# Reversed columns in 512-column matmuls and interleaved halves of the pair products' weights

## The chip, the core and the metric

The kernel runs on one core of one Trainium2 chip. The metric is the device time of one execution in microseconds (us); lower is better. Five engines of the core work side by side, each with its own stream of instructions: TensorE (PE, with its weight loads as PEld) multiplies, VectorE (DVE) and ScalarE (ACT) do elementwise work, GpSimd (POOL) does small things, SyncE (SP) issues most transfers (DMA). SBUF is the on-chip working memory, PSUM the memory into which TensorE writes its sums; both have 128 partitions. PSUM is used here as eight banks of 512 fp32 columns per partition.

A matmul here is two instructions: LDWEIGHTS loads a 128 x 128 block (the weights) into the array, MATMUL streams the other operand (the moving one) through it, column by column, and adds the results to columns of PSUM. In Python it is one call, `nc.tensor.matmul(out, weights, moving, ...)`.

## The reference

Two requests of 512 tokens with 1024 features each go through the same trunk of two layers and a final RMSNorm:

```python
for i in range(DEPTH):                        # DEPTH = 2
    h = rms_norm(x, norm_g[i], NORM_EPS)
    if i % N_MIXERS == 0:
        x = x + diff_attention(h, da_w_in[j], ..., da_w_out[j], lambda_init)
    else:
        x = x + bidir_retention(h, ret_w_in[j], ..., ret_w_out[j])
return rms_norm(x, final_norm_g, NORM_EPS)
```

Layer 1 is differential attention: `proj = h @ w_in` (1024 x 8192) gives queries and keys of 16 half heads, values and a gate; the queries and keys are rotated; each of the 8 heads takes the difference of two softmaxes times the values, a norm, the gate, and `@ w_out` (2048 x 1024). Layer 2 is retention in both directions with decays: a projection of 1024 x 6144, rotation, a masked product by chunks, norm, gate and an output projection of 2048 x 1024. All in fp32.

## The kernel before, in words

**Numbers.** A value is split into a rounded part (hi, in the type fp32r, which TensorE multiplies in one pass) and the rest (lo). `hi_of` (L399) makes the first on ScalarE with a copy that casts (L400), `lo_of` (L402) the second on VectorE with a subtraction (L403). A product then takes three matmuls, hi with hi, hi with lo and lo with hi: `PASSES` (L32).

**Projections into the heads.** They are computed with Strassen and Winograd's scheme of seven products of half matrices instead of eight. The transposed and normed activations of both requests are the B operands (`make_b`, L448): tiles `[128, 2, 512]`, hi and lo, which stay in SBUF, some in a large tile `arena` and some in tiles `b`. The projection's weights are the A operands. A `Unit` (L518) is 256 columns of them. `prep` (L551) loads them from HBM into `raw` tiles, combines them as the product asks (L558, into `st`), and splits the result into hi and lo in a `ws` tile; there are seven places for `ws` tiles. `product` (L586) issues the matmuls, `evac` (L627) copies, adds and stores the results.

There are two kinds of units. In a *wide* unit (the values) the activations are the loaded 128 x 128 blocks and the weights are the moving operand, in 256 columns (L609). In a *pair* unit (queries, keys, gates) it is the other way round: the block loaded into the array is 128 columns of the projection's weights, and the activations are the moving operand, all 512 tokens of a request, into a whole bank (`pair`, L596 to L601). One pair product is four k blocks times three passes, 12 matmuls. Its `ws` tile is `[P, 2, 4, n]` (L578): all of hi, then all of lo, each as four blocks of 128 columns. For the queries and keys the weights of a unit are picked by `half_view` (L944) in layer 1 and by `parity_view` (L947, every second column) in layer 2.

**Attention, retention, output.** `scores` (L1107) multiplies queries by keys, 512 key columns in three matmuls per half head (L1116). `av` (L1170) and its like in layer 2 (L1359, L1367, L1315, L1339) have 256 columns. `out_step` (L871) is the output projection: the weighted values are the loaded blocks, 512 columns of the output weights the moving operand, six matmuls to a bank (L891); VectorE adds the bank to the residual (L896). The very last step is done in two halves of 256 columns. Transposes (L606, L716, L815, L1028, L1161) are matmuls by the identity.

**Order.** All of it is recorded first, with a cost for each operation, and `Plan.arrange` (L138) then simulates the engines with these costs, picks for each engine what it issues next, and fixes the order; `Plan.issue` (L232) issues it. The planner knows costs by engine and size, not the direction or step of an access. Places in SBUF are given out by `slot` (L303), which shifts some tiles by 16 or 32 elements.

Of the kernel before, what the change touches and what calls it, by code (L numbers as in the profile page):

```python
# [15 lines left out]
P = 128  # L16
# [237 lines left out]
def trunk_kernel(  # L254
# [7 lines left out]
    nc = tc.nc  # L262
# [34 lines left out]
    def work(tag, shape, bufs, dt=F32, name=None):  # L297
        size = SIZE.get(tag, shape[1])
        return Buf(plan, tag, bufs, lambda i: view(wk, tag, i, size, shape, dt))
# [27 lines left out]
    def ws_t(shape):  # L327
        return work("ws", shape, WS_BUFS, F32R)
# [4 lines left out]
    def st_t(shape, name="st"):  # L333
        return work("st", shape, 3, name=name)
# [18 lines left out]
    def bank(tag, name=None):  # L353
        return Buf(plan, tag, BUFS[tag], lambda i: view(pj if tag == "pj" else sc, tag, i, S, [P, S]))
# [16 lines left out]
    def dve(n, fn, r, w, wait=0.0):  # L371
        plan.op("DVE", 0.07 + 0.00104 * n, fn, r, w, wait=wait)

    def axpy(n, fn, r, w):

        plan.op("DVE", 0.13 + 0.00104 * n, fn, r, w)
# [13 lines left out]
    def pe(cost, fn, r, w, wait=0.0):  # L390
        plan.op("PE", cost, fn, r, w, wait=wait)
# [7 lines left out]
    def hi_of(n, dst, src, r, w):  # L399
        act(n, lambda: nc.scalar.copy(dst(), src()), r, w)  # L400

    def lo_of(n, dst, src, hi, r, w):  # L402
        dve(n, lambda: nc.vector.tensor_tensor(dst(), src(), hi().bitcast(F32), op=ALU.subtract), r, w)  # L403
# [114 lines left out]
    class Unit:  # L518
# [32 lines left out]
        def prep(self, op):  # L551
            x = self.take
            n = 256 if self.wide else P

            def combine(a, b, fn):
                t = st_t([P, 4, n])
                out = ((lambda: self.like(t.t)), t)
                dve(4 * n, lambda: nc.vector.tensor_tensor(out[0](), a[0](), b[0](), op=fn), [a[1], b[1]], [t])  # L558
                return out
            if op == "P1":  # L560
                src = x(0, 0)
            elif op == "P2":
                src = x(0, 1)
            elif op == "P4":
                src = x(1, 1)
            elif op == "P5":
                src = self.s[1] = combine(x(1, 0), x(1, 1), ALU.add)
            elif op == "P6":
                src = self.s[2] = combine(self.s[1], x(0, 0), ALU.subtract)
            elif op == "P3":  # L570
                src = combine(x(0, 1), self.s[2], ALU.subtract)
            else:
                src = combine(x(0, 0), x(1, 0), ALU.subtract)
            if self.wide:
                a, b = ws_t([P, 4, n]), ws_t([P, 4, n])
                hi, lo = ((lambda: a.t), a), ((lambda: b.t), b)
            else:
                s = ws_t([P, 2, 4, n])  # L578
                hi, lo = ((lambda: s[:, 0]), (s, 0)), ((lambda: s[:, 1]), (s, 1))
            hi_of(4 * n, lambda: self.like(hi[0]()), src[0], [src[1]], [hi[1]])  # L580
            lo_of(4 * n, lambda: self.like(lo[0]()), src[0], lambda: self.like(hi[0]()), [src[1], hi[1]], [lo[1]])
            self.ops[op] = (hi, lo)
            if op == "P2" and self.early is not None:
                self.early, self.x = None, {}

        def product(self, op):  # L586
            which = BANK_OF[op]
            n_banks = 2 if self.wide else 1
            opens = op in OPENS
            if opens:  # L590
                self.banks[which] = [bank(self.tags[which], which) for _ in range(n_banks)]
            a, b = self.ops.pop(op), B_OF[op]
            bt = [Bop[b, k] for k in range(4)]
            reads = [q[1] for q in a] + bt

            def pair(ps, ks=range(4)):  # L596
                for k in ks:
                    for i, (u, v) in enumerate(PASSES):
                        nc.tensor.matmul(  # L599
                            ps.t, a[u][0]()[:, k, :], bt[k][:, v, :], start=(opens and k == 0 and i == 0),  # L600
                            stop=(k == 3 and i == 2), skip_group_check=True)  # L601

            def wide(ps, t):
                if self.led and op == "P1" and t == 0:
                    for j in range(NT):
                        nc.tensor.transpose(ps[:, j * P:(j + 1) * P], ident.t, ident.t)  # L606
                for k in range(4):
                    for i, (u, v) in enumerate(PASSES):
                        nc.tensor.matmul(  # L609
                            ps[:, (t % 2) * 256:(t % 2) * 256 + 256], bt[k][:, v, t * P:(t + 1) * P],  # L610
                            a[u][0]()[:, k, :], start=(opens and t % 2 == 0 and k == 0 and i == 0),
                            stop=(k == 3 and i == 2), skip_group_check=True)

            if not self.wide:
                ps = self.banks[which][0]
                if op == "P1" and self in first_units[:2]:
                    for k in range(4):
                        pe(0.7, lambda k=k: pair(ps, (k,)), reads[:2] + [bt[k]], [(ps, k)])
                else:
                    pe(2.79, lambda: pair(ps), reads, [ps])  # L620
                return
            for t in range(NT):
                ps = self.banks[which][t // 2]
                led = self.led and op == "P1" and t == 0
                pe(1.87 if led else 1.43, lambda ps=ps, t=t: wide(ps, t), reads + [ident] * led, [ps])
# [236 lines left out]
    def out_weights(w, h, i):  # L862
        r = raw_t([P, 2, S])
        src = w[h * 256:(h + 1) * 256, i * S:(i + 1) * S].rearrange("(e p) c -> p e c", p=P)
        dma(lambda: r.t, lambda: src, [], [r], 512)
        hi, lo = ws_t([P, 2, S]), ws_t([P, 2, S])
        hi_of(1024, lambda: hi.t, lambda: r.t, [r], [hi])
        lo_of(1024, lambda: lo.t, lambda: r.t, lambda: hi.t, [r, hi], [lo])
        wsn[h, i] = (hi, lo)

    def out_step(w, h, g, t, i, o, rr, last, parts=1):  # L871


        owed[h, g] -= 1
        if (h, i) not in wsn:
            out_weights(w, h, i)
        banks = [bank("pj") for _ in range(parts)]
        u = wsn[h, i]
        x = xN[g, t]
        n = S // parts  # L880
        for p in range(parts):
            here = slice(p * n, (p + 1) * n)
            part = (x, i) if parts == 1 else (x, (i, p))

            ps = banks[p]

            def fn(here=here, ps=ps):
                m = 0
                for e in range(2):
                    for a, b in PASSES:  # L890
                        nc.tensor.matmul(ps[:, here], o[a][:, e, t * P:(t + 1) * P], u[b][:, e, here],  # L891
                                         start=(m == 0), stop=(m == 5))
                        m += 1
            pe(1.39 / parts, fn, [(o[0], t // 2), (o[1], t // 2), *u], [ps])
            half = x[:, i * S + p * n:i * S + (p + 1) * n]
            axpy(n, lambda half=half, here=here, ps=ps: nc.vector.scalar_tensor_tensor(  # L896
                half, ps[:, here], rr[:, t % 2:t % 2 + 1], half, op0=ALU.mult, op1=ALU.add),
                [ps, part, rr], [part])
            if h == NH - 1:
                last(g, t, i, half, n, part, i == 1 and p == parts - 1)  # L900
# [206 lines left out]
    def scores(i):  # L1107
        h, g, t = tiles[i]
        st[i]['s'] = []
        for j in range(2):  # L1110
            s = bank("sc")
            q, k = qk[h, g, j, 0], qk[h, g, j, 1]

            def fn(s=s, q=q, k=k):
                for n, (a, b) in enumerate(PASSES):
                    nc.tensor.matmul(s.t, q[:, a, t * P:(t + 1) * P], k[:, b, :], start=(n == 0), stop=(n == 2))  # L1116
            pe(0.7, fn, [q, k], [s])
            st[i]['s'].append(s)

# [333 lines left out]
    for i in range(N2 + 1):  # L1453
        if i < N2:
            b, c = chunks[i]
# [78 lines left out]
```

## Time and profile before

| what | value |
|---|---|
| median of 3 runs | 1808.89 us (1808.3 to 1814.46) |
| span of the profiled execution, first to last instruction | 1807.0 us |
| the profiled execution's own time | not listed apart; the median is 1.9 us over its span |
| instructions | 27780 |
| granted TensorE clock, mean | 0.999 |
| moved by DMA | 328.81 MB, mean 182 GB/s |

The page lists busy time by engine, the span in 40 slices with a digit for the busy tenths of each, then shares of the chain of work that ended last, and the costliest groups of instructions. In a group, "128*128 128x512" is a 128 x 128 loaded block and 512 moving columns, xN is how many instructions, then come the busy time in us and the mean duration of one in ns, and after the second bar how long its engine sat idle before them. Matmuls overlap: one starts while the one before it drains. The timeline gives start, length and count of runs of equal instructions in us; the chain in order of time gives start and length of each piece. SBUF places do not show in a profile.

### The profile page before, as it was taken

To read this page: it belongs to the slowest core of one execution; us is meant where nothing else is said; L and a number is where in the kernel's file an instruction comes from. 1 tells how busy PE (TensorE), PEld (TensorE's weight loads), DVE (VectorE), ACT (ScalarE), POOL (GpSimd) and SP (SyncE) were. 2 spreads that over 40 slices of the span, in tenths; PEclk is the share of its full clock that TensorE was granted. 3 is DMA by queue.
4 is the path that set the end of the run, shared out by engine and by line. 5 is a ranking of instruction groups with operands and counts; after the bars stand their busy time and mean duration, and the time that the engine had idled before them with its cause. 6 is when DMAs were issued, how large, how long until landed. Compare 5 with 4: busy or idle time off the path is not lost.

```text
span 1807.0 us, 27780 instructions
## 1 busy us (share of the span) xinstructions
PE 1794.9 (99%) x10299; PEld 1558.1 (86%) x10299; DVE 1477.1 (82%) x2319; ACT 895.1 (50%) x1856; POOL 169.5 (9%) x323
## 2 busy tenths in 40 slices
PE   9999999999999999999999999999999999999998
PEld 6789889898988888888888888898989898888887
DVE  7958787778699888888888897787887967888887
ACT  7753444433434565554555866444434355444346
POOL 1000000000000022222322300000000000111113
PEclk9999999999999999999999999999999999999999
DMA  6444455555545685444554524464657559765662
GB/s 217 134 126 137 161 140 178 184 168 155 174 126 175 201 334 198 178 156 159 190 204 140 190 73 146 140 210 146 205 156 228 151 170 396 272 238 182 225 218 94
DMA packets 162767, 328.81 MB, mean 182 GB/s; under 512 B 12724, under 2 KB 76872, under 8 KB 162632
## 3 DMA queue, kind: packets, MB, share of 16 engines
q1 hardware_dynamic: 162304, 326.71, 54.1%
q8 instruction: 81, 1.33, 0.3%
q14 instruction: 54, 0.44, 0.1%
q10 hardware_dynamic: 328, 0.34, 0.1%
HBM read 209.55 MB, written 117.44 MB: 181 GB/s over the span
## 4 chain that ended last, share of the span: by engine, by line
PE 93%; DVE 2%; DMA 2%; ACT 2%; issue 1%; POOL 0%; SPq 0%; POOLq 0%; DVEq 0%; ACTq 0%
PE pj L599 20%; PE pj L891 19%; PE sc L599 10%; PE pj L609 10%; PE o L599 8%; PE o L1181 5%; PE sc L1116 5%; PE sc L609 5%; PE o L609 2%; PE o L1359 2%; PE tp L1161 2%; PE sc L1315 1%; PE o L1367 1%; PE tp L1339 1%; DMA raw<-in_ret_w_out_dram 1%
## 5 line engine op out<-in xcount | busy, mean ns | idle before, releaser
L891 PE MATMUL pj<-ws,arena 128*128 128x512 f32 x1542 | 391.2, 397 | 0.0
L891 PEld LDWEIGHTS pj<-ws,arena 128*128 128x128 f32 x1542 | 277.7, 188 | 52.7
L599 PE MATMUL pj<-b,ws 128*128 128x512 f32 x1080 | 265.0, 392 | 0.0
L599 PEld LDWEIGHTS pj<-b,ws 128*128 128x128 f32 x1080 | 201.4, 188 | 43.0
L403 DVE TENSOR_TENSOR ws<-st,ws 128x512 fp32r<-128x512 f32 (+1 forms) x192 | 147.9, 774 | 74.8 <-ACT ws L400 56.7
L896 DVE SCALAR_TENSOR_TENSOR b<-pj,crr,b 128x512 f32<-128x512 f32 (+1 forms) x257 | 189.9, 744 | 21.4 <-PE pj L891 21.0
L403 DVE TENSOR_TENSOR ws<-raw,ws 128x512 fp32r<-128x512 f32 (+1 forms) x164 | 141.5, 868 | 71.3 <-ACT ws L400 61.0
L400 ACT CAST ws<-st 128x512 fp32r<-128x512 f32 (+1 forms) x192 | 132.4, 693 | 121.4 <-PE pj L599 36.4
L599 PE MATMUL sc<-arena,ws 128*128 128x512 f32 x768 | 186.8, 392 | 0.0
L599 PE MATMUL o<-arena,ws 128*128 128x512 f32 x744 | 180.0, 393 | 1.1 <-ACT m L385 0.6
L599 PEld LDWEIGHTS sc<-arena,ws 128*128 128x128 f32 x768 | 144.0, 188 | 31.3
L400 ACT CAST ws<-raw 128x512 fp32r<-128x512 f32 (+1 forms) x164 | 125.7, 772 | 87.0 <-PE o L599 45.0
L599 PEld LDWEIGHTS o<-arena,ws 128*128 128x128 f32 x744 | 138.4, 188 | 31.7 <-DVE arena L463 1.4
L599 PE MATMUL pj<-arena,ws 128*128 128x512 f32 x648 | 160.3, 392 | 0.4 <-DVE arena L463 0.4
L599 PEld LDWEIGHTS pj<-arena,ws 128*128 128x128 f32 x648 | 120.8, 188 | 26.7 <-DVE arena L463 0.7
L1134 ACT ACTIVATE b<-sc,nm 128x512 f32<-128x512 f32 x128 | 88.0, 689 | 66.9 <-DVE nm L1124 66.5
L636 ACT COPY c<-pj 128x512 f32<-128x512 f32 x104 | 60.9, 586 | 119.7 <-PE pj L599 66.4
L609 PE MATMUL pj<-ws,b 128*128 128x256 f32 x960 | 116.8, 276 | 0.0
L609 PEld LDWEIGHTS pj<-ws,b 128*128 128x128 f32 x960 | 113.2, 188 | 0.7
L1116 PE MATMUL sc<-arena 128*128 128x512 f32 x384 | 101.2, 395 | 0.3 <-ACT b L1134 0.3
L1181 PEld LDWEIGHTS o<-arena 128*128 128x128 f32 x768 | 93.1, 188 | 2.7
L1181 PE MATMUL o<-arena 128*128 128x256 f32 x768 | 93.7, 278 | 0.0
(207 smaller groups left out, 2855.9 us busy)
## 6 DMA issues: line engine op xcount, KB each, us to landing
qk<-os SPq DMA_DIRECT2D x192, 256.0 KB, 3.6
arena<-qk SPq DMA_DIRECT2D x96, 512.0 KB, 5.8
raw<-in_da_w_in_dram SPq DMA_DIRECT2D x64, 512.0 KB, 5.1
v<-os SPq DMA_DIRECT2D x64, 512.0 KB, 4.3
arena<-v SPq DMA_DIRECT2D x64, 512.0 KB, 4.1
raw<-in_ret_w_in_dram SPq DMA_DIRECT2D x48, 512.0 KB, 4.8
os<-g SPq DMA_DIRECT2D x32, 512.0 KB, 7.4
g<-e SPq DMA_DIRECT2D x48, 256.0 KB, 4.6
```

The costliest lines, as they stand in the source:

```text
L400: act(n, lambda: nc.scalar.copy(dst(), src()), r, w)
L403: dve(n, lambda: nc.vector.tensor_tensor(dst(), src(), hi().bitcast(F32), op=ALU.subtract), r, w)
L599: nc.tensor.matmul(ps.t, a[u][0]()[:, k, :], bt[k][:, v, :], start=(opens and k == 0 and i == 0), stop=(k == 3 and i == 2), skip_group_che ...
L609: nc.tensor.matmul(ps[:, (t % 2) * 256:(t % 2) * 256 + 256], bt[k][:, v, t * P:(t + 1) * P], a[u][0]()[:, k, :], start=(opens and t % 2 == ...
L636: act(S, lambda c=c, ps=ps: nc.scalar.copy(c.t, ps.t), [ps], [c])
L891: nc.tensor.matmul(ps[:, here], o[a][:, e, t * P:(t + 1) * P], u[b][:, e, here], start=(m == 0), stop=(m == 5))
L896: axpy(n, lambda half=half, here=here, ps=ps: nc.vector.scalar_tensor_tensor(half, ps[:, here], rr[:, t % 2:t % 2 + 1], half, op0=ALU.mult ...
L1116: nc.tensor.matmul(s.t, q[:, a, t * P:(t + 1) * P], k[:, b, :], start=(n == 0), stop=(n == 2))
L1134: act(840, lambda j=j, s=s, m=m: nc.scalar.activation(p[:, j, :], s.t, AF.Exp, bias=m.t, accum_out=sm[:, 2 * j + n:2 * j + n + 1]), [s, m] ...
L1161: nc.tensor.transpose(tp[:, j * P:(j + 1) * P], p[:, 0, j * P:(j + 1) * P], ident.t)
L1181: nc.tensor.matmul(o[:, e * 256:(e + 1) * 256], v[b][:, j, e * P:(e + 1) * P], aT[a][:, j, :], start=(n == 0), stop=(n % 12 == 11), skip_g ...
L1359: nc.tensor.matmul(o[:, e * 256:(e + 1) * 256], v_[v][:, 2 * c + j, e * P:(e + 1) * P], a_[:, u, j * 256:(j + 1) * 256], start=(e == 0 and ...
```

## The change

Three places of matmuls with 512 moving columns now give the moving operand and the PSUM output with `[::-1]`: column 511 is read first and its result is written to column 511. Every column still lands where it did. The 256-column matmuls elsewhere stay as they were (the two halves of the last output step, which share a line with the 512-column ones, are reversed with them). And the `ws` tile of a pair product is `[P, 4, n, 2]` instead of `[P, 2, 4, n]`: hi and lo of an element stand next to each other, so ScalarE writes hi and VectorE writes lo at every second element, and a weight load reads 128 columns at a step of two elements. Wide units keep their two separate tiles.

```diff
@@ -575,8 +575,8 @@
             else:
-                s = ws_t([P, 2, 4, n])
-                hi, lo = ((lambda: s[:, 0]), (s, 0)), ((lambda: s[:, 1]), (s, 1))
+                s = ws_t([P, 4, n, 2])
+                hi, lo = ((lambda: s[:, :, :, 0]), (s, 0)), ((lambda: s[:, :, :, 1]), (s, 1))
@@ -597,7 +597,7 @@
                         nc.tensor.matmul(
-                            ps.t, a[u][0]()[:, k, :], bt[k][:, v, :], start=(opens and k == 0 and i == 0),
+                            ps[:, ::-1], a[u][0]()[:, k, :], bt[k][:, v, ::-1], start=(opens and k == 0 and i == 0),
                             stop=(k == 3 and i == 2), skip_group_check=True)
@@ -888,7 +888,7 @@
-                        nc.tensor.matmul(ps[:, here], o[a][:, e, t * P:(t + 1) * P], u[b][:, e, here],
+                        nc.tensor.matmul(ps[:, here][:, ::-1], o[a][:, e, t * P:(t + 1) * P], u[b][:, e, here][:, ::-1],
                                          start=(m == 0), stop=(m == 5))
@@ -1113,7 +1113,8 @@
-                    nc.tensor.matmul(s.t, q[:, a, t * P:(t + 1) * P], k[:, b, :], start=(n == 0), stop=(n == 2))
+                    nc.tensor.matmul(s[:, ::-1], q[:, a, t * P:(t + 1) * P], k[:, b, ::-1],
+                                     start=(n == 0), stop=(n == 2))
```

From L1117 on, line numbers of the changed kernel are one higher.

## The prediction

> **What bounds the kernel now.** I read the page's first two parts, then the chain's shares, then the costliest groups, and last how far apart the matmuls start.
>
> ```profile
> span 1807.0 us, 27780 instructions
> ...
> PE 1794.9 (99%) x10299; PEld 1558.1 (86%) x10299; DVE 1477.1 (82%) x2319; ACT 895.1 (50%) x1856; POOL 169.5 (9%) x323
> ...
> PEclk9999999999999999999999999999999999999999
> ...
> PE 93%; DVE 2%; DMA 2%; ACT 2%; issue 1%; POOL 0%; SPq 0%; POOLq 0%; DVEq 0%; ACTq 0%
> ```
>
> TensorE is busy 1794.9 of 1807.0 us, its clock is granted in full in every slice, and it makes 93% of the chain that ended last. So the time is the sum of the starts of one matmul after another, and little else. These are the groups that the edit touches, from the costliest groups and (the one of x120) the groups by form:
>
> ```profile
> L891 PE MATMUL pj<-ws,arena 128*128 128x512 f32 x1542 | 391.2, 397 | 0.0
> L599 PE MATMUL pj<-b,ws 128*128 128x512 f32 x1080 | 265.0, 392 | 0.0
> L599 PEld LDWEIGHTS pj<-b,ws 128*128 128x128 f32 x1080 | 201.4, 188 | 43.0
> L599 PE MATMUL sc<-arena,ws 128*128 128x512 f32 x768 | 186.8, 392 | 0.0
> L599 PE MATMUL o<-arena,ws 128*128 128x512 f32 x744 | 180.0, 393 | 1.1 <-ACT m L385 0.6
> L599 PE MATMUL pj<-arena,ws 128*128 128x512 f32 x648 | 160.3, 392 | 0.4 <-DVE arena L463 0.4
> L1116 PE MATMUL sc<-arena 128*128 128x512 f32 x384 | 101.2, 395 | 0.3 <-ACT b L1134 0.3
> L599 PE MATMUL sc<-b,ws 128*128 128x512 f32 x120 | 29.1, 391 | 0.0
> ```
>
> Together 1542 + 1080 + 768 + 744 + 648 + 384 + 120 = 5286 matmuls, 3360 of them pair products (L599). Idle before them is about nothing. The 392 ns are not the price of one: the next starts while it drains. The price is the step from start to start, which the chain in order of time and the timeline of TensorE show:
>
> ```profile
> 75.27 8.24 PE pj L599 x36
> ...
> 1089.36 8.24 PE pj L599 x36
> ```
> ```profile
> 297.71 5.63 PE L609 MATMUL o<-ws,arena 128*128 128x256 f32 x48
> 303.18 5.60 PE L609 MATMUL sc<-ws,arena 128*128 128x256 f32 x48
> ```
>
> In the chain, 36 pair matmuls take 8.24 us in both layers: **a step of 229 ns for 512 columns**. In the timeline, 48 matmuls of 256 columns take 303.18 - 297.71 = 5.47 us: a step of 114 ns, each with its own weight load. So a load needs at most 114 ns of throughput (its 188 ns overlap the next), and under a 512-column matmul 229 - 114 = 115 ns of load time are free.
>
> **What the step is made of.** Two places of one line, in the timeline of TensorE:
>
> ```profile
> 807.27 1.56 PE L1116 MATMUL sc<-arena 128*128 128x512 f32 x6
> 808.67 0.60 PE L1161 MATMUL tp<-ident,b 128*128 128x128 f32 x4
> ```
> ```profile
> 819.42 1.54 PE L1116 MATMUL sc<-arena 128*128 128x512 f32 x6
> 820.79 0.60 PE L1161 MATMUL tp<-ident,b 128*128 128x128 f32 x4
> ```
>
> The same six score matmuls take 1.40 us at one place (233 ns each) and 1.37 us at the other (228 ns). Line, shapes and neighbours are the same and only the places in SBUF differ. So 5 ns of a step depend on where the operands lie. That is my reading: the weight load of the next matmul and the running matmul's moving stream sometimes want the same part of SBUF. The Trainium skill (TensorE: Matmul & The Clock Gate, Part 2, "Step-by-step: what each phase is for") says otherwise: the two have independent read ports, and loading the next weights takes no bandwidth from the running matmul. By that rule the edit changes no step; the 233 against 228 ns above do not agree with it.
>
> **The change part by part.** It adds no instruction, and each engine issues the same work in the same order, the transfers too; the planner's costs are untouched. What changes is the walk through memory.
>
> (a) *Moving data and PSUM from last column to first*, 5286 matmuls. No row of before shows a stream in this direction, so I bound it. From above in cost: every column takes its slot twice, 229 ns more each (below, as a rival). From below: the step could fall to two of the shortest load steps.
>
> ```profile
> 863.63 0.25 PEld L815 LDWEIGHTS o<-ident,m 128*128 128x128 f32 x2
> ```
> ```profile
> L1161 PEld LDWEIGHTS tp<-ident,b 128*128 128x128 f32 x256 | 31.4, 140 | 7.8 <-DVE b L1150 0.4
> ```
>
> Two loads for transposes, each of 140 ns as the second row has it, end 0.25 us after the first started: 0.11 us apart, and two of these are 220 ns. No row shows a shorter 512-column step, so I take 220 ns as the low end: 9 ns under 229.
>
> (b) *Weights of pair products interleaved*, 3360 loads, now at a step of two elements: 128 columns lie over 1024 bytes instead of 512. No row shows such a load. It has 115 ns of cover: even if it took twice its 114 ns of throughput (228), it would just fit a 229 ns step. I cost it at nothing; without the cover, each 10 ns over it would be 34 us. But it changes the pace: 1024 bytes in 114 ns are 9.0 bytes/ns, and the moving stream walks 2048 bytes in 229 ns, 8.9 bytes/ns. Before, the load walked at 4.5 and the stream overtook it. If the load goes from the last column to the first as the stream now does, the two keep a fixed distance and do not meet; the trace cannot show its direction. **This is the step on which my forecast rests.**
>
> (c) *ScalarE and VectorE write the halves at a step of two*, VectorE reads one of them so. Groups by form, the first over the whole span, then the same casts in two stretches, 150 to 650 us (whose weights are read without a step of two) and 1100 to 1500 us (where the rotary weights are read with one, L947):
>
> ```profile
> L403 DVE TENSOR_TENSOR ws<-st,ws 128x512 fp32r<-128x512 f32 x160 | 108.9, 685 | 56.7 <-ACT ws L400 56.2
> ...
> L403 DVE TENSOR_TENSOR ws<-raw,ws 128x512 fp32r<-128x512 f32 x108 | 73.1, 685 | 24.3 <-ACT ws L400 18.2 <-PE pj L609 5.6
> ...
> L403 DVE TENSOR_TENSOR ws<-b,ws 128x512 fp32r<-128x512 f32 x12 | 7.9, 680 | 0.0
> ```
> ```profile
> L400 ACT CAST ws<-raw 128x512 fp32r<-128x512 f32 x51 | 31.3, 622 | 40.1 <-PE o L599 22.5 <-PE pj L599 7.9 <-PE pj L609 5.2
> ```
> ```profile
> L400 ACT CAST ws<-raw 128x512 fp32r<-128x512 f32 x35 | 22.2, 646 | 30.9 <-PE o L599 19.5 <-PE pj L609 5.2 <-PE sc L599 2.8
> ```
>
> A read at a step of two costs a cast 24 ns in the mean, if it is the cause. A write at that step is shown nowhere: from nothing up to twice the time, 160 + 108 + 12 = 280 times 0.69 = 192 us of VectorE. Most of that would lie in VectorE's 1807.0 - 1477.1 = 330 us of idle, but not in the start:
>
> ```profile
> 19.00:56.00 37.00, 35.10 (x166) 27.84 (x165) 36.52 (x59) 29.43 (x54) 4.82 (x8) 1.00 0.35 114
> 56.00:146.00 90.00, 90.00 (x395) 73.85 (x394) 69.28 (x110) 51.23 (x87) 0.00 (x0) 1.00 0.43 133
> ```
>
> By stages (busy TensorE, loads, VectorE, ScalarE, GpSimd), VectorE fills 36.52 of the 37 us up to 56 us and sets the pace there; from then on TensorE is never idle. Some 13 of the 280 subtractions lie in that stage: doubled, 13 x 0.68 = 9 us. I take nothing, by the cheap reads. The Trainium skill (SBUF — State Buffer, "Door 1: The DMA port swizzle") holds that SBUF is reached in lines of 16 bytes and that two hits per line keep full rate, which a step of two still has; by it too the sum stays.
>
> **The sum.** Pair products from 229 to 220 ns, less about 110 of them in the stage that VectorE sets: 3250 x 9 = 29 us. The other 1926 get only the direction; their loads still walk at half the pace, so I take half of the gain: 1926 x 4.5 = 9 us. Together 38. What is late next: around 1500 us the chain in order of time waits for transfers, and a TensorE that comes there sooner gives some back; I take 4 us of the 18.
>
> ```profile
> 1498.25 10.58 DMA raw<-in_ret_w_out_dram
> 1508.85 1.05 ACT ws L400
> 1510.31 7.85 DMA g<-e
> ```
>
> 38 - 4 = 34 us: a span of 1773. The median of the runs, 1808.89, is 1.9 us over the span; added, **1775 us**.
>
> **The rivals.**
>
> *Nothing happens (1809).* The direction is not seen by either memory, and the 229 ns are the stream's own pace. For it: 229 is twice 114 within 1 ns, so 512 columns may simply cost what two times 256 do. Against it: the 233 and 228 ns above.
>
> *The streams now meet more often (1835): slower.* If the load goes from the first column up, the reversed stream runs against it and crosses it in every matmul. Its price is the bad place of L1116 for all: 5 ns x 5286 = 26 us, 1809 + 26. It decides from a mean step of 231 ns on (9 us, 0.5%, over 5286). For it: that row shows that such a state exists. Against it: most steps are at 229 now, so the bad state is the rarer.
>
> *The reversed stream loses its pace (about 3020): slower.* If the memory merges neighbouring columns only upwards, each column takes its own access: 229 x 5286 = 1210 us more. The Trainium skill (PSUM — Partial Sum Buffer, "Specifications (TRN2)") warns of it: lines of 8 bytes, and any access that is not contiguous slows matmuls a good deal. By that rule it would decide here; whether minus one counts as contiguous it does not say. For it in the trace: nothing, no row runs downwards. Against it: neither, except that a line of two columns is still used twice in a row.
>
> *Strided writes are dear (1818).* The 9 us of (c).
>
> **How the numbers follow.** A run here tells about 0.5% (9 us) from no change. Forecast, faster: 0.48 (from 220 ns steps everywhere and a little more, 1750, to just over 9 us, 1800). Nothing: 0.17. Meeting more often: 0.20. Lost pace: 0.10. Dear writes: 0.05. So faster 0.48, same 0.17, slower 0.35. The range goes from 1740 to 1845: it takes in the forecast, nothing, the meeting streams and the writes up to ten us over their prices, and leaves out the lost pace (0.10), 0.05 below and a few hundredths of the worse collisions. The forecast's own range is 1750 to 1800.
>
> **What would show it.** In the profile after: the chain's pieces of 36 pair matmuls should last 7.9 us instead of 8.24; L1116's six 1.35; L609's 48 stay at 5.47. L400 and L403 on ws at 128x512 stay at 620 to 650 and 685 ns. If the 36 still take 8.24, (a) and (b) do nothing; at 8.3 to 8.5 the streams meet; at 16 the pace is lost. If the loads of L599 last well over 188 ns and the step grows with them, (b) has run out of cover. The forecast is wrong above all if the 229 ns are the stream's own pace.

## The result and the profile after

The changed kernel takes 1837.87 us (median of 4 runs, 1834.78 to 1840.87); the kernel before took 1808.71 us beside it (4 runs, 1808.3 to 1814.46). The ratio is 1.0154, interval 1.0133 to 1.0175: **slower by 29 us**, where I had forecast 1775. The profiled execution took 1834.78 us. Its page begins so:

```profile
span 1832.9 us, 27785 instructions
...
PE 1820.9 (99%) x10299; PEld 1587.3 (87%) x10299; DVE 1480.8 (81%) x2319; ACT 907.6 (50%) x1856; POOL 170.2 (9%) x323
...
PEclk9999999999999999999999999999999999999999
...
PE 93%; DVE 2%; DMA 2%; ACT 1%; issue 0%; POOL 0%; SPq 0%; POOLq 0%; ACTq 0%; DVEq 0%
```

The same 10299 matmuls, the same clock, the same share of the chain. The span is 25.9 us longer and TensorE is busy 26.0 us more: nothing waits longer, the matmuls themselves stand further apart. The chain in order of time (start, length, what) gives the step, in both layers:

```profile
75.66 8.40 PE pj L599 x36
...
301.66 5.44 PE o L609 x48
...
1100.48 8.40 PE pj L599 x36
...
1191.86 5.65 PE o L609 x48
...
1519.35 10.52 DMA raw<-in_ret_w_out_dram
```

36 pair matmuls take 8.40 us instead of 8.24: 8.40 / 36 = **233.3 ns a step instead of 228.9**. And the wide products of L609, which the change does not touch, take 5.44 us in layer 1 (113.3 ns) but 5.65 in layer 2 (117.7). The wait for the output weights has its old length (10.52 after 10.58 us) and comes 21.1 us later. The page's groups say the same in mean durations (the last number before the second bar, in ns):

```profile
L891 PE MATMUL pj<-ws,arena 128*128 128x512 f32 x1542 | 395.8, 401 | 0.0
...
L599 PE MATMUL pj<-b,ws 128*128 128x512 f32 x1080 | 269.6, 397 | 0.0
L599 PEld LDWEIGHTS pj<-b,ws 128*128 128x128 f32 x1080 | 208.8, 195 | 40.3
...
L1116 PE MATMUL sc<-arena 128*128 128x512 f32 x384 | 102.6, 399 | 0.3 <-ACT b L1135 0.3
```

Each of the three edited lines has matmuls 4 to 5 ns longer (397, 392 and 395 before). The interleaved loads take 195 ns instead of 188; their reading at a step of two costs 7 ns each, under a step of 233.

For the comparisons below I added up the distances from each matmul's start to the next one's start, by line, out of the traces (us; lines of before; "distance" is that of the work tiles' beginning to that of the operand slots and the arena, modulo 128 bytes, as the built kernels place them, which leaves aside that `slot` shifts some tiles by 64 or 128 bytes; L891 is without its halves of 256 columns; the last column is the time of the run or its median, while the sums of "after" come from its execution of 1834.78 us):

```
kernel                          distance   L599   L609   L891  L1116    time
before                             64     774.3  305.7  360.8   89.8  1808.7
after                              64     788.0  310.9  365.2   91.1  1837.9
reversal alone                     64     788.4  305.4  365.2   91.1  1829.7
moving operand reversed alone      64     788.5  305.4  365.2   91.1  1830.1
PSUM reversed alone                64     774.2  305.7  360.9   89.8  1809.1
interleaving alone                 64     788.2  316.2  360.8   89.8  1832.8
before, work tiles 32 B lower      32     788.4  317.6  364.0   90.3  1840.1
before, slots, arena 32 B higher   32     788.5  317.6  364.0   90.3  1840.3
before, all tiles 32 B lower       64     775.4  305.9  360.8   89.8  1810.2
before, work tiles 64 B lower       0     785.0  319.9  360.1   90.4  1837.9
reversal, work tiles 64 B lower     0     788.0  320.5  365.4   91.1  1844.6
interleaving, same                  0     782.5  319.8  360.1   90.3  1835.1
after, same                         0     788.3  319.4  365.4   91.1  1843.7
```

After against before: 13.7 + 5.1 + 4.4 + 1.3 = 24.5 of the 25.9 us of span lie in these four lines; the next, L1359, has 1.4. The kernel before, the changed one, the reversal alone and the interleaving alone ran four times or more, every other kernel once. Rows with the same edit and the same distance agree within 0.3 us in L599, but for the one with all tiles 32 bytes lower (1.1 us more, at a granted clock of 0.998 instead of 0.999).

### The profile page after: what moved, and what is told of

The parts are those of the page before. It is cut to its first block, busy times and chain, and to the rows that moved or that the text cites. A ratio compares the mean times of both kernels' runs of the same rounds, so it can differ in the third digit from the quotient of the medians.

```text
span 1832.9 us, 27785 instructions
## 1 busy us (share of the span) xinstructions
PE 1820.9 (99%) x10299; PEld 1587.3 (87%) x10299; DVE 1480.8 (81%) x2319; ACT 907.6 (50%) x1856; POOL 170.2 (9%) x323
## 4 chain that ended last, share of the span: by engine, by line
PE 93%; DVE 2%; DMA 2%; ACT 1%; issue 0%; POOL 0%; SPq 0%; POOLq 0%; ACTq 0%; DVEq 0%
PE pj L599 20%; PE pj L891 19%; PE sc L599 11%; PE pj L609 10%; PE o L599 8%; PE sc L1116 5%; PE sc L609 5%; PE o L1182 5%; PE o L609 2%; PE o L1360 2%; PE tp L1162 2%; PE o L1368 1%; PE sc L1316 1%; PE tp L1340 1%; DMA raw<-in_ret_w_out_dram 1%; DVE ws L403 1%
## 5 line engine op out<-in xcount | busy, mean ns | idle before, releaser
L891 PE MATMUL pj<-ws,arena 128*128 128x512 f32 x1542 | 395.8, 401 | 0.0
L891 PEld LDWEIGHTS pj<-ws,arena 128*128 128x128 f32 x1542 | 278.1, 188 | 55.8
L599 PE MATMUL pj<-b,ws 128*128 128x512 f32 x1080 | 269.6, 397 | 0.0
L599 PEld LDWEIGHTS pj<-b,ws 128*128 128x128 f32 x1080 | 208.8, 195 | 40.3
L400 ACT CAST ws<-st 128x512 fp32r<-128x512 f32 (+1 forms) x192 | 141.2, 740 | 131.3 <-PE pj L599 31.7
L599 PE MATMUL sc<-arena,ws 128*128 128x512 f32 x768 | 190.2, 397 | 0.0
L599 PE MATMUL o<-arena,ws 128*128 128x512 f32 x744 | 183.2, 398 | 1.0 <-ACT m L385 0.6
L400 ACT CAST ws<-raw 128x512 fp32r<-128x512 f32 (+1 forms) x164 | 131.0, 805 | 92.4 <-PE o L599 42.6
L599 PEld LDWEIGHTS sc<-arena,ws 128*128 128x128 f32 x768 | 149.3, 195 | 29.5
L599 PEld LDWEIGHTS o<-arena,ws 128*128 128x128 f32 x744 | 143.4, 195 | 29.9 <-DVE arena L463 1.3
L599 PE MATMUL pj<-arena,ws 128*128 128x512 f32 x648 | 163.2, 397 | 0.3 <-DVE arena L463 0.3
L599 PEld LDWEIGHTS pj<-arena,ws 128*128 128x128 f32 x648 | 125.2, 195 | 25.1 <-DVE arena L463 0.6
L609 PE MATMUL pj<-ws,b 128*128 128x256 f32 x960 | 118.8, 279 | 0.0
L609 PEld LDWEIGHTS pj<-ws,b 128*128 128x128 f32 x960 | 115.0, 188 | 0.7
L1116 PE MATMUL sc<-arena 128*128 128x512 f32 x384 | 102.6, 399 | 0.3 <-ACT b L1135 0.3
```

The source lines that it names most:

```text
L599: nc.tensor.matmul(ps[:, ::-1], a[u][0]()[:, k, :], bt[k][:, v, ::-1], start=(opens and k == 0 and i == 0), stop=(k == 3 and i == 2), skip ...
L609: nc.tensor.matmul(ps[:, (t % 2) * 256:(t % 2) * 256 + 256], bt[k][:, v, t * P:(t + 1) * P], a[u][0]()[:, k, :], start=(opens and t % 2 == ...
L891: nc.tensor.matmul(ps[:, here][:, ::-1], o[a][:, e, t * P:(t + 1) * P], u[b][:, e, here][:, ::-1], start=(m == 0), stop=(m == 5))
L1116: nc.tensor.matmul(s[:, ::-1], q[:, a, t * P:(t + 1) * P], k[:, b, ::-1], start=(n == 0), stop=(n == 2))
```

## The experiments

The theory after the result was the slower rival of the prediction: the reversed stream meets the loads more often. Against it stood that the reversed writes into PSUM cost, that the interleaved loads do, or that the strided writes of ScalarE and VectorE disturb TensorE. The first four kernels take the change apart.

**Reversal without interleaving.**

```diff
-    ps.t, a[u][0]()[:, k, :], bt[k][:, v, :], ...          # L599, and L891, L1116 alike
+    ps[:, ::-1], a[u][0]()[:, k, :], bt[k][:, v, ::-1], ...
```

> All three sites reversed, moving data and PSUM, the pair products' weights as before (all of hi, then all of lo). Theory A (the direction costs: the reversed stream meets the next weight load more often): 512-column steps at 233 ns at all three lines as in the changed kernel, about 1830 us or more. Theory B (the interleaved load costs: its 195 ns against 188 delay the next matmul): pair steps back at 229 ns, casts on ScalarE back at 621 ns, 1809 to 1815 us. Theory C (a matter of phase between the engine and its memories that any edit may tip): anything, and then the unchanged 256-column matmuls move too.

Measured: 1829.69 us, ratio 1.0112 (1.0095 to 1.0129). Its chain in order of time:

```profile
1100.78 8.40 PE pj L599 x36
...
1192.16 5.44 PE o L609 x48
```

The whole rise of the pair step, 228.9 to 233.3, is there without any interleaving, L891 and L1116 have risen as in the whole change, and L609 is untouched in both layers. So **the reversal alone takes the pair products to where the whole change has them**; on top of it the interleaving gives them nothing.

**Interleaving without reversal.**

```diff
-    s = ws_t([P, 2, 4, n])
+    s = ws_t([P, 4, n, 2])     # and hi, lo as in the change
```

> Pair products' weights interleaved, every matmul in the old direction. Theory A: steps of 229 ns at L599, L891 and L1116, loads of 195 ns that nothing waits for, casts at 678 ns, 1809 us within 5. Theory B: pair steps at 233 ns, L891 and L1116 as before, about 1825 us. The write at a step of two costs a cast 57 ns by both, hidden.

Measured: 1832.76 us, ratio 1.013 (1.0115 to 1.0145). The chain in order of time:

```profile
303.58 5.65 PE o L609 x48
...
1104.22 8.40 PE pj L599 x36
...
1195.48 5.65 PE o L609 x48
```

The pair step is 233.3 here too, and L609, neither edited nor moved, goes from 113.3 to 117.7 in both layers: 316.2 - 305.7 = 10.5 us. The two edits are not additive, 21 and 24 us alone and 29 together: either one lengthens the pair products by 14 us, and both together do so by no more. The sums agree but the patterns do not: from one pair matmul to the next the starts go 233, 233, 234 ns with the reversal alone, 236, 231 with the whole change, and 230, 236, 235, 232 with the interleaving alone. So that the same thing happens in all three is not shown.

**Which half of the reversal.** The moving operand alone, then the PSUM output alone, at the same three places.

```diff
-    ps.t, a[u][0]()[:, k, :], bt[k][:, v, :], ...
+    ps.t, a[u][0]()[:, k, :], bt[k][:, v, ::-1], ...        # moving operand alone
+    ps[:, ::-1], a[u][0]()[:, k, :], bt[k][:, v, :], ...    # PSUM alone
```

> No interleaving; the moving operand is read from the last column to the first but the result is written to PSUM from the first column on, so the columns of scores, projections and outputs come out in the wrong order (data alone, no instruction is left out). Theory A (SBUF is where the streams meet): steps as in the run with both reversed, 233 ns. If writing PSUM downwards is what costs: 229 ns.

> No interleaving; the moving operand is read upwards as before, the result is written to PSUM from the last column to the first, so its columns come out in the wrong order (no instruction is left out). Theory A: 229 ns, the time of the kernel before. If writing PSUM downwards costs: 233 ns and about 1830 us.

Measured: 1830.13 us with the moving operand reversed, 1809.12 us with PSUM reversed. The chain of the PSUM one:

```profile
1089.60 8.24 PE pj L599 x36
...
1179.29 5.47 PE o L609 x48
```

**Writing PSUM downward costs nothing**: 8.24 and 5.47 us as before. All of the reversal's price comes from reading the moving operand downward. The Trainium skill (PSUM — Partial Sum Buffer, "Specifications (TRN2)") says that any access that is not contiguous slows matmuls a good deal; a step of minus one, as this run has it, does not.

That leaves a question. In the kernel before the pair steps are not even: within a product they go 226, 229, 232, again and again, and with the reversal alone 233, 233, 234. I took such exact repetition as a sign that other engines' traffic does not make it. And L609 has two values, 113.3 and 117.7, with the same operands in the same places. New theory: 233 and 118 are the usual steps, and the kernel before stands by its layout at a favourable one that both edits lose. Rival: reading downward, and loading at a step of two, each have a price of their own at any place.

**The places alone.** The arena has 80 spare elements; with fewer, everything behind it, the work tiles (`ws`, `raw`, `st` and the small ones), moves down. Nothing else changes: the kernel before, the reversal and the whole change with the work tiles 64 bytes lower, and the kernel before with them 32 bytes lower.

```diff
-    arena = ar.tile([P, 18 * 1024 + 80], ...)
+    arena = ar.tile([P, 18 * 1024 + 64], ...)   # 64 bytes lower; + 72: 32 bytes lower
```

> The kernel before with the pool of work tiles (ws among them) 64 bytes lower, by a smaller arena in front of it; arena and activations stay. No access pattern changes. Theory A (a matter of place: load and moving stream meet according to their distance in SBUF): steps of L599, L609 and L891 change, pair steps to 233 ns or some other value, L1116, whose operands both lie in the arena, stays at 228 to 233. Theory D (only direction and step of an access count): 229, 114 and 231 ns as before, 1809 us.

> Reversal alone (moving data and PSUM, no interleaving) with the work pool 64 bytes lower. Theory A: the distance is another, so pair and L891 steps leave 233 ns, perhaps back to 229; L1116 stays at 233. Theory D: 233 ns at all three, 1830 us.

> The whole change with the work pool 64 bytes lower. Theory A: pair steps leave 233 ns. Theory D: as the changed kernel, 1834 to 1840 us.

> The kernel before with the work pool 32 bytes lower: its tiles then start on a multiple of 64 bytes, the arena's still 32 behind one. Theory A: L599, L609 and L891 take other steps than 229, 114 and 231 ns, L1116 does not. If what costs is a start in the middle of a 64 byte line, L609 (moving operand in the pool) gets shorter. Theory D: no change.

Measured: 1837.92, 1844.62, 1843.73 and 1840.08 us. The chain of the kernel before with its work tiles 64 bytes lower, and then 32 bytes lower:

```profile
75.90 8.37 PE pj L599 x36
...
165.70 5.69 PE o L609 x48
```
```profile
166.05 5.70 PE o L609 x48
...
1106.67 8.40 PE pj L599 x36
...
1198.11 5.63 PE o L609 x48
```

**A shift of 32 bytes, with every instruction as it was, costs 31 us**, about as much as the whole change. With the work tiles 32 bytes lower the pair products have nearly the sum of the changed kernel (788.4 against 788.0), with them 64 bytes lower a little less (785.0), and L609 goes to between 117.3 and 118.8 ns. The theory had L1116 stay, as both of its operands lie in the arena; it rises by 0.5 us in both (89.8 to 90.3 and 90.4). The rival is half right, though: the reversed stream has 788.0 to 788.5 at both places tried, where the theory had it leave 233 ns, and at the second place it still costs 3 us in the pair products and 5.3 in L891.

**Distance or alignment.** Two more moves of the kernel before. A constant of 4 bytes put behind the work tiles lets everything above it slide down 32 bytes; 32 bytes of padding ahead of the slots, with 32 fewer in the arena, raise all but the work tiles.

```diff
-    pool = sm
+    pool = tail if tag == "minus1" else sm              # all 32 bytes lower
```
```diff
+    sm.tile([P, 8], F32, tag="pad", name="pad")         # slots and arena 32 bytes higher
-    arena = ar.tile([P, 18 * 1024 + 80], ...)
+    arena = ar.tile([P, 18 * 1024 + 72], ...)
```

> The kernel before with one 4-byte constant (minus1) moved behind the work tiles, so that everything above it in SBUF (operand slots, arena and work tiles alike) lies 32 bytes lower; the distances between the operands of all matmuls stay as they were, their alignment to 64 bytes does not. The theory that the distance between moving operand and weights sets the step: 1809 us, pair products at 228.9 ns and L609 at 113.3 ns, as before. The rival, that alignment sets it (all operands of the kernel before lie 32 bytes off a multiple of 64; these lie on one): 1838 to 1842 us, pair products at about 233.3 and L609 at about 118, as where the work tiles alone were moved by 32 bytes.

> The kernel before with operand slots, arena and constants 32 bytes higher and the work tiles where they were: their distance is the one of the run with the work tiles 32 bytes lower (32 modulo 128), the alignments are not. If the distance alone sets the steps: that run's values again, pair products at 233.3 with its pattern (231, 231, 238), L609 at 118.7 and 117.4, and 1840 us. If the alignment of one of the two operands sets them: other steps, near 229 and 113 if it is that of the work tiles.

Measured: 1810.24 us, with 1810.22 for the kernel before beside it, and 1840.26 us. The two chains, first that with all tiles 32 bytes lower (line numbers are one higher in both):

```profile
165.12 5.46 PE o L610 x48
...
1090.80 8.24 PE pj L600 x36
```
```profile
165.63 5.70 PE o L610 x48
...
1106.34 8.40 PE pj L600 x36
...
1197.79 5.63 PE o L610 x48
```

With slots, arena and work tiles moved together nothing changes, though each now begins on another multiple of 32 bytes. With the other side of the distance moved, the time of the shift by 32 comes back, and with it every sum of its row to 0.2 us. So **in these kernels the step follows the distance between the two groups of tiles, not the alignment of either**. Two things stay open: whether the distance counts modulo 128 bytes, and whether it is TensorE's two reads that meet, as the work tiles also hold what ScalarE, VectorE and the transfers write.

**Interleaving at another distance.** The interleaved kernel without reversal, its work tiles 64 bytes lower.

```diff
-    arena = ar.tile([P, 18 * 1024 + 80], ...)   # in the kernel with interleaving alone
+    arena = ar.tile([P, 18 * 1024 + 64], ...)
```

> The interleaved weights alone (no reversal), with the work tiles 64 bytes lower. If the interleaved load sets the pair step whatever the place, as the reversed stream does: pair products at 233 to 234 ns as at the old place, L609 at 118 to 119, L891 near 360 us in sum, and 1838 to 1845 us in all. If interleaving only loses a favourable place, some other place may be favourable to it: pair products below 230 ns, and a time below 1832 us.

Measured: 1835.12 us. Its chain and its loads:

```profile
75.89 8.33 PE pj L599 x36
```
```profile
L599 PEld LDWEIGHTS pj<-b,ws 128*128 128x128 f32 x1080 | 209.8, 196 | 37.5
```

Neither expectation holds as written: the pair step is 8.33 / 36 = 231.4 ns, between the two. But against its own neighbour, the kernel before at that place (8.37, 785.0 us), the interleaving gains 2.5 us in the pair products, with loads of 196 ns. At the old place it cost 13.9. So a price of its own at any place, as the rival had it, is not there: at one of the two distances tried the interleaved load costs, at the other it gains.

**Is L609's step handed on?** The interleaved kernel at the old place, with four transposes of the identity ahead of each wide product that opens a bank (and the planner told of their cost).

```diff
-    if self.led and op == "P1" and t == 0:
+    if opens and t == 0:
         for j in range(NT):
             nc.tensor.transpose(ps[:, j * P:(j + 1) * P], ident.t, ident.t)
```

> The interleaved weights alone (no reversal), at the old place, with four transposes of the identity into the bank ahead of each wide product that opens one (P1, P5, P2 of every wide unit), as the kernel has them ahead of its first. They cost about 0.45 us each time, some 10 us in all. If the 117.8 ns of L609, which this edit doesn't touch, are a state handed on from the matmuls before: the steps behind the added transposes change to the 115.5 ns that the first wide product has behind its transposes in both kernels, or to 113.3, and stay so until the next pair product. If they come from something that goes on beside TensorE (the strided writes of ScalarE and VectorE, transfers): 117.8 stays behind the transposes too.

Measured: 1837.26 us, 4.5 over the interleaved kernel (92 more transposes of about 0.1 us each, and L609 4.3 us shorter). The chain in order of time; the first three rows stand directly behind transposes, the fifth behind a pair product:

```profile
166.56 5.66 PE o L609 x48
...
305.25 5.46 PE o L609 x48
311.14 5.47 PE sc L609 x48
316.61 5.44 PE pj L609 x48
...
335.74 5.66 PE pj L609 x48
...
1210.18 5.44 PE pj L609 x48
```

In two of the four units of layer 1 and in the four of layer 2, L609 falls from 117.8 to 113.3 ns behind the transposes and stays there for the 240 matmuls up to the next pair product; behind that it is at 117.8 again. In the other two units of layer 1 (the first row) the transposes leave it at 117.8. The strided writes and the transfers go on in all of them, and no operand has moved. So **the step of these unedited matmuls is a state that they take over from what ran before them**; what goes on beside TensorE does not hold it there. What decides which state a sequence falls into was not found.

No version here beats the kernel before: of the distances tried (64, 32, 0) its own is the best, and of the edits to the matmuls only the reversed write into PSUM comes free.

## Why the prediction was wrong

**What bounds the kernel: right; what a step is made of: in part.** TensorE's steps are the time; it is busy 99% in every kernel above, and the spans differ by the sums of the steps. That some 5 ns of a step can hang on the operands' places shows in the pair products: 32 bytes of distance move them by 14.1 us, 4.2 ns a step. It does not show in L1116, from which I had read it. The second of its two places in the prediction took 1.37 us for six matmuls. With only the work tiles moved, 64 bytes lower, the same six, both of whose operands stay where they were in the arena, behind the same 24 of L1181, take 835.36 - 833.96 = 1.40 us:

```profile
833.96 1.56 PE L1116 MATMUL sc<-arena 128*128 128x512 f32 x6
835.36 0.60 PE L1161 MATMUL tp<-ident,b 128*128 128x128 f32 x4
```

So the step of L1116 goes from 228 to 233 ns with its own operands in their old places. My sentence that only places differ between 233 and 228 ns overlooked what such matmuls may take over from earlier ones, as L609 does. The rule of the Trainium skill that I set against it (TensorE: Matmul & The Clock Gate, Part 2, "Step-by-step: what each phase is for": loading the next weights takes nothing from the running matmul) does not account for these steps; a step that depends on the distance of the two groups of tiles speaks for the two reads disturbing each other. That they do, and that it is the same part of SBUF that both want, remains an argument, as no profile shows SBUF's insides.

**The step that failed is (b)**, "If the load goes from the last column to the first as the stream now does, the two keep a fixed distance and do not meet", on which I said the forecast rests. In its place: interleaved and reversed, the pair products step at 233.3 ns, the same as reversed alone (788.0 against 788.4 us), so with the reversal in place the interleaving brought the pair products nothing. Whether the load walks the other way, so that the two cross, or an equal pace is of no use, no run separates. Without reversal the interleaving costs 13.9 us or gains 2.5, by the distance. I had taken the kernel before for a middling case that a better walk could improve. Of the layouts tried it was the favourable one: its walk of 4.5 against 8.9 bytes/ns steps at 228.9 ns, and each other walk of the operands and each other distance tried steps higher.

**(a)** fell as well, in size and sign: I took 9 ns off a step, down to 220; the reversed read adds 4.4 ns to a pair step. Pair products had a mean step below 228.9 ns in no kernel. The half gain for L891 and L1116, 9 us, is a loss of 4.4 + 1.3 = 5.7 us. My reason against the slower rival, that most steps are at 229 now and the bad state is rarer, counted states of one layout as if they were drawn by chance.

**(c) was right**, beyond its durations. Groups of the changed kernel by form:

```profile
L403 DVE TENSOR_TENSOR ws<-st,ws 128x512 fp32r<-128x512 f32 x160 | 109.3, 687 | 61.1 <-ACT ws L400 61.0
L400 ACT CAST ws<-st 128x512 fp32r<-128x512 f32 x160 | 107.6, 678 | 81.2 <-PE pj L599 25.1 <-issue 13.1 <-PE sc L599 11.4
```

VectorE's subtractions stay at 687 ns (685 before). ScalarE's casts take 678 ns, above the 620 to 650 I expected, and the difference is hidden: the first run of 36 pair matmuls begins at 75.66 us, and at 75.91 in the kernel with reversal alone, whose casts are not strided. The load's 195 ns against 188 had its cover, as costed; that this is no loss by itself shows in the interleaved kernel at the second place. The Trainium skill (SBUF — State Buffer, "Door 1: The DMA port swizzle") would have a step of two at full rate; these loads take 7 ns more.

**The rivals.** "The streams now meet more often (1835)" named the time and its range held it, but only part of its sum: 5 ns for all 5286 edited matmuls was 26 us, and they gave 13.7 + 4.4 + 1.3 = 19.4. The rest came from L609 (5.1) and lines of 256 columns behind it, which nobody edited. That the total came out near it is luck. And its mechanism, a reversed stream that crosses a load, is not needed: the interleaving alone and a shift of 32 bytes alone do as much. It is not ruled out for the reversed stream either. "Lost pace" is out (8.40, not 16), "dear writes" too, and "nothing" holds for PSUM's half alone.

**What stays open.** What in TensorE or its memories makes a step 233 instead of 229 ns, why the reversed stream has the same 233 ns at both places tried, which way a load walks through its columns (a reversed load was not tried), and what sets L609's state. The four runs of the changed kernel lie at 1834.78, 1835.02, 1840.71 and 1840.87 us; L609 of layer 1 in its other state would be 1344 x 4.5 ns = 6.0 us, which fits, but no profile of the longer ones was taken.

## What to carry to other kernels

Where TensorE bounds a kernel with a weight load for every matmul, the distance in SBUF between the tiles of the weights and those of the moving operand is worth a trial of its own: here 32 bytes were worth 31 us in 1809. So before a change of an access pattern, or of any tile's size, is credited or blamed, move the tiles with nothing else changed and see what that alone does. And compare the steps of lines that the change did not touch: if they move too, as L609 did here, part of the price does not come from the edited access itself.

## What the runs showed of the hardware

- Reading a moving operand of 512 fp32r columns downward steps at 233.3 ns, upward at 228.9 to 233.3 by the distance to the weights; writing PSUM downward costs nothing (1809.12 against 1809.2 us).
- Matmuls of 256 columns, each with its load, step at 113.3 or 117.8 ns with the same operands in the same places, and keep to one of the two until other matmuls come between. Six of 512 columns (L1116) step at 228 or 233 ns with their own operands in the same places, when only other tiles move.
- ScalarE's cast of 512 elements that writes at a step of two takes 661 (interleaving alone) to 678 ns (the whole change) instead of 620 (reversal alone); VectorE's subtraction 687 instead of 685; a weight load at a step of two 195 to 196 instead of 188.
